# Scores of the last query tile made for both maps together, in two PSUM tiles

## The chip, the cores and the metric

The kernel runs on one core of a Trainium2 chip. The metric is the device time of one execution in microseconds (us), as the median of several runs. Five engines work side by side and wait for each other through semaphores: TensorE (PE in the profile; its weight loads are PEld), VectorE (DVE), ScalarE (ACT), GpSimd (POOL) and SyncE (SP), which issues most transfers.

## What is computed

Two transformer-like blocks over a sequence of 512 positions (528 with 16 meta tokens) of width 1024. The change is in the first block's differential attention: 8 heads, and in each head two softmax maps over the same values, with a key and a query of 64 channels for each map.

```python
def block(i):                       # i: a tile of 128 queries
    qb = lax.dynamic_slice_in_dim(qf, start, QB, axis=1)
    ...
    s = jnp.einsum('bqhmd,bkhmd->bhmqk', qb, kf)          # m: the map, d: 64 channels
    mask = cid[None, :] <= qc[:, None]
    p = jax.nn.softmax(jnp.where(mask, s, NEG_INF), axis=-1)
    a = p[:, :, 0] - lam * p[:, :, 1]
    return jnp.einsum('bhqk,bkhe->bqhe', a, vf)
```

Around it stand the projections that make queries, keys, values and gates, a causal convolution of 31 taps with a layer norm, output products, a feed-forward part, and then a second block of other mixers.

## The kernel before

All is held transposed: channels on partitions, positions along the free axis. The matrix products of the projections are the main stream of PE: units of 8 steps, and in a step 6 products (`step`, L560: three of the split weights by two column ranges of 256 to 264) accumulate into a tile `mm` of PSUM. There are two `mm` tiles. 56 such units make the first block's mixer, and the next weights are loaded and split into two parts (`wh` by ACT, `wl` by DVE) while a unit runs.

All else in the first mixer is side work. It is written as generators that run against a planner's clock (`self.pe`, and a lane each for DVE and ACT): after each step of the main stream `tick` resumes each generator whose time has come, and what it issues lands between two steps. The order is fixed when the program is built. A generator asks with `due` when its input will be ready by the plan and sleeps till then. A product in float32 is charged 4 columns in a cycle of 2.4 GHz by the plan (`mm`), whatever rows it uses. Operations of the convolution are taken from a list as DVE has room by the plan.

Side work has two PSUM tiles of 1024 columns, `at0` and `at1`. `at_get` hands out the one that is free by the plan, and `at_put` gives it back.

A head is two generators. `first` runs `softmax(i)` for the query tiles i = 0 to 3 (up to two ahead of use). `second` turns the values, and for each query tile combines the two maps (`weigh`), turns the result (`turn`, 128x128 blocks against `ident`) and multiplies with the values (`values`). Map 0 lies on partitions 0 to 63 of the queries and keys, map 1 on 64 to 127, so each score product uses 64 rows. For i = 0, 1 and 2 both maps fit into one tile: map m is written from column 512 m on, the product of map 0 and then that of map 1, and one memset and one reduction treat both. For i = 3 there are 528 key positions, which in two maps exceed one tile. There each map takes a tile by itself, with two products of 264 columns:

```python
for m in range(2):
    i_at, pt = yield from self.at_get()
    mm(pt[:, 248:512], q(m), k(m, 0, 264), True, True)
    mm(pt[:, 512:776], q(m), k(m, 264, 528), True, True)
    yield self.due(pt)
    V.memset(pt[0:64, 712:776], NEG)
    V.tensor_reduce(nb[:, m : m + 1], pt[:, 248:776], axis=AX.X, op=MAX, negate=True)
    yield self.due(nb)
    ex(m, pt[:, 248:776])
    self.at_put(i_at)
```

`ex` is the exponential on ACT with the row sum. In the profile the lines of DVE and ACT are all L158 (a helper), products are L314, and turns (products with `ident`) are L320; score products are `at<-act 64*128`, where 64 is the number of rows.

Of the kernel before, what the change touches and what calls it, by code (L numbers as in the profile page):

```python
# [52 lines left out]
def free(ap):  # L53
    n = 1
    for d in ap.shape[1:]:
        n *= d
    return n
# [105 lines left out]
class Build:  # L163
# [141 lines left out]
    def mm(self, out, lhsT, rhs, start=True, stop=True):  # L305
        n = free(rhs)
        if rhs.dtype == F32:
            c = max(0.213, n * 4 / 2400)
        elif rhs.dtype == F32R:
            c = max(0.107, n / 2400 + 0.003)  # L310
        else:
            c = max(0.03, n / 2400)
        self.pe_op(c, out, [lhsT, rhs])
        self.nc.tensor.matmul(out, lhsT, rhs, start=start, stop=stop)  # L314
# [448 lines left out]
    def attention(self, tp, h, qk, vs, ctx):  # L763


        V, S, mm, tr = self.V, self.S, self.mm, self.tr
# [3 lines left out]
        k = lambda m, a, b: kT[64 * m : 64 * m + 64, a:b]  # L770
        pair = lambda pt: pt.rearrange("p (a n) -> p a n", a=2)

        def softmax(i):
            L = 144 + 128 * i
            q = lambda m: qT[64 * m : 64 * m + 64, 2 + 128 * i : 130 + 128 * i]
            nb, l = self.sm(2, "nb"), self.sm(1, "ll")
            e = self.slot()

            def ex(m, sv):
                S.activation(e[:, m, :L], sv, AF.Exp, bias=nb[:, m : m + 1], accum_out=l if m else l0[:, i : i + 1])  # L780

            yield self.due(qT)
            if i < 3:
                i_at, pt = yield from self.at_get()
                for m in range(2):
                    mm(pt[:, 512 * m : 512 * m + L], q(m), k(m, 0, L))
                if i == 0:
                    for m in range(2):
                        mm(pt[0:2, 512 * m + 256 : 512 * m + 272], qT[64 * m : 64 * m + 64, 0:2], k(m, 0, 16))
                yield self.due(pt)  # L790
                V.memset(pair(pt)[0:64, :, L - 64 : L], NEG)
                if i == 0:
                    V.tensor_copy(sx[:, h, :, :], pair(pt)[0:2, :, 256:272])
                    if h == 7:
                        state["heads"] = True
                V.tensor_reduce(nb, pair(pt)[:, :, :L], axis=AX.X, op=MAX, negate=True)
                yield self.due(nb)
                for m in range(2):
                    ex(m, pt[:, 512 * m : 512 * m + L])
                self.at_put(i_at)  # L800
            else:
                for m in range(2):
                    i_at, pt = yield from self.at_get()
                    mm(pt[:, 248:512], q(m), k(m, 0, 264), True, True)
                    mm(pt[:, 512:776], q(m), k(m, 264, 528), True, True)
                    yield self.due(pt)
                    V.memset(pt[0:64, 712:776], NEG)
                    V.tensor_reduce(nb[:, m : m + 1], pt[:, 248:776], axis=AX.X, op=MAX, negate=True)
# [3 lines that stand above are left out]
            return e, l  # L812

        def first():
            for i in range(4):
                while i >= used[0] + 2:
                    yield 0.2
                made.append((yield from softmax(i)))
# [1384 lines left out]
```

## Time and profile before

| | |
|---|---|
| median of 3 runs | 1579.39 us (1579.03 to 1579.42) |
| the profiled execution | 1577.79 us |
| its span (first to last instruction) | 1576.0 us |
| granted TensorE clock, mean | 0.999 of full speed |
| PE busy | 1557.2 us, 99% |
| DVE busy | 1100.9 us, 70% |
| ACT busy | 680.3 us, 43% |
| 16 DMA engines, mean rate | 85 GB/s |

The busy time of PE is a union of instructions that overlap: one product is still draining when the next one starts. How long a product holds the engine is read from one start to the next, not from its own duration. The side work of the eight heads lies between 77 and 461 us of the span.

### The profile page before, as it was taken

To read this page: it belongs to the slowest core of one execution; us is meant where nothing else is said; L and a number is where in the kernel's file an instruction comes from. 1 tells how busy PE (TensorE), PEld (TensorE's weight loads), DVE (VectorE), ACT (ScalarE), POOL (GpSimd) and SP (SyncE) were. 2 spreads that over 40 slices of the span, in tenths; PEclk is the share of its full clock that TensorE was granted. 3 is DMA by queue.
4 is the path that set the end of the run, shared out by engine and by line. 5 is a ranking of instruction groups with operands and counts; after the bars stand their busy time and mean duration, and the time that the engine had idled before them with its cause. 6 is when DMAs were issued, how large, how long until landed. Compare 5 with 4: busy or idle time off the path is not lost.

```text
span 1576.0 us, 25330 instructions
## 1 busy us (share of the span) xinstructions
PE 1557.2 (99%) x10281; PEld 1392.9 (88%) x10281; DVE 1100.9 (70%) x2011; ACT 680.3 (43%) x1222; POOL 26.5 (2%) x89
## 2 busy tenths in 40 slices
PE   7999999999999999999999999999999999999998
PEld 6999999999999999999988877797799888888886
DVE  4989999897764667767643357899768877775224
ACT  5344444446843344444332222635566544444122
POOL 4000000000000000000000000000000000000000
PEclk9999999999999999999999999999999999999999
DMA  5322222222222333233333332231054133333221
GB/s 144 95 68 69 78 70 70 75 59 67 81 69 67 108 94 92 85 93 94 91 88 89 91 102 76 68 108 54 1 147 121 53 95 94 94 94 107 94 94 67
DMA packets 233005, 134.17 MB, mean 85 GB/s; under 512 B 6925, under 2 KB 228240, under 8 KB 232888
## 3 DMA queue, kind: packets, MB, share of 16 engines
q1 hardware_dynamic: 231448, 130.35, 28.5%
q8 instruction: 81, 1.33, 0.3%
q0 software_dynamic: 1136, 1.15, 0.3%
q10 hardware_dynamic: 304, 1.05, 0.2%
q14 instruction: 36, 0.29, 0.1%
HBM read 130.44 MB, written 2.10 MB: 84 GB/s over the span
## 4 chain that ended last, share of the span: by engine, by line
PE 97%; DVE 1%; ACT 1%; DMA 0%; issue 0%; DVEq 0%; ACTq 0%; POOLq 0%
PE mm L314 70%; PE at L314 25%; PE at L320 3%; ACT act L158 1%; DMA act<-in_x_dram 0%; DVE act L158 0%; DVE yy L158 0%; DVE yc L158 0%; ACT ys L158 0%; DVE wl L158 0%; DVE fx L158 0%; DVE res L158 0%; DVEq L2199 0%; ACT rsy L158 0%; DVE rsy L158 0%
## 5 line engine op out<-in xcount | busy, mean ns | idle before, releaser
L314 PE MATMUL mm<-act,wh 128*128 128x256 f32 (+3 forms) x4720 | 907.9, 306 | 1.3 <-ACT act L158 0.5
L314 PEld LDWEIGHTS mm<-act,wh 128*128 128x128 f32 (+1 forms) x4720 | 692.1, 189 | 50.5 <-issue 11.9
L314 PE MATMUL mm<-act,wl 128*128 128x256 f32 (+4 forms) x2360 | 562.6, 302 | 0.0
L158 DVE TENSOR_TENSOR wl<-raw,wh 128x1024 fp32r<-128x1024 f32 (+2 forms) x235 | 284.5, 1211 | 174.3 <-ACT wh L158 171.8
L158 ACT ACTIVATE wh<-raw 128x1024 fp32r<-128x1024 f32 (+2 forms) x235 | 245.7, 1047 | 371.4 <-PE mm L314 191.5
L314 PEld LDWEIGHTS mm<-act,wl 128*128 128x128 f32 (+1 forms) x2360 | 383.5, 189 | 18.0
L158 DVE SCALAR_TENSOR_TENSOR act<-u,par,act 128x514 f32<-128x514 f32 x232 | 161.2, 748 | 2.2 <-ACT act L158 2.2
L314 PE MATMUL at<-act,wh 128*128 128x512 f32 x416 | 129.6, 392 | 0.0
L314 PEld LDWEIGHTS at<-act,wh 128*128 128x128 f32 x416 | 78.0, 188 | 18.3
L314 PE MATMUL at<-wh,act 128*128 128x512 f32 x264 | 85.8, 394 | 0.0
L314 PE MATMUL mm<-wh,act 128*128 128x256 f32 (+1 forms) x344 | 84.6, 320 | 0.0
L314 PE MATMUL at<-act,act 128*128 128x256 f32 (+9 forms) x468 | 83.6, 329 | 0.7 <-ACT act L158 0.6
L314 PE MATMUL at<-act,wl 128*128 128x512 f32 x208 | 81.9, 394 | 0.0
L158 DVE TENSOR_TENSOR act<-act,act 128x514 f32<-128x514 f32 (+4 forms) x122 | 69.7, 590 | 9.0 <-ACT act L158 8.3
L314 PEld LDWEIGHTS at<-act,act 128*128 128x128 f32 (+1 forms) x468 | 60.3, 189 | 11.1 <-issue 5.0
L158 DVE SCALAR_TENSOR_TENSOR ft<-fx,par,ft 128x512 f32<-128x512 f32 x88 | 65.8, 749 | 1.5
L158 DVE TENSOR_TENSOR fx<-mm,rB 128x514 f32<-128x514 f32 x44 | 30.5, 694 | 51.3 <-PE mm L314 50.6
L158 ACT ACTIVATE act<-mm 128x528 f32<-128x528 f32 (+2 forms) x64 | 35.1, 548 | 71.7 <-PE mm L314 71.6
L314 PEld LDWEIGHTS mm<-wh,act 128*128 128x128 f32 x344 | 58.0, 189 | 7.2 <-issue 3.4
L158 DVE SCALAR_TENSOR_TENSOR gy<-gx,par,gy 128x512 f32<-128x512 f32 x84 | 62.6, 749 | 1.5
L158 ACT ACTIVATE act<-at 128x128 f32<-128x128 f32 (+6 forms) x88 | 34.3, 411 | 58.8 <-PE at L314 41.3
L314 PEld LDWEIGHTS at<-wh,act 128*128 128x128 f32 x264 | 49.6, 188 | 11.3
(286 smaller groups left out, 1450.7 us busy)
## 6 DMA issues: line engine op xcount, KB each, us to landing
raw<-in_w_in_dram SPq DMA_DIRECT2D x82, 512.0 KB, 3.8
raw<-in_w_up_dram SPq DMA_DIRECT2D x44, 512.0 KB, 3.8
raw<-in_ffn_up_dram SPq DMA_DIRECT2D x44, 512.0 KB, 3.8
raw<-in_ffn_down_dram SPq DMA_DIRECT2D x22, 512.0 KB, 3.3
raw<-in_w_out_dram SPq DMA_DIRECT2D x20, 512.0 KB, 4.5
raw<-in_w_down_dram SPq DMA_DIRECT2D x16, 512.0 KB, 3.8
raw<-in_w_conv_out_dram SPq DMA_DIRECT2D x8, 512.0 KB, 3.8
raw<-in_w_down_dram SPq DMA_DIRECT2D x8, 384.0 KB, 3.4
```

What stands on the lines that cost most here:

```text
L158: return f(*a, **k)
L314: self.nc.tensor.matmul(out, lhsT, rhs, start=start, stop=stop)
L320: self.nc.tensor.transpose(out, src, self.ident[p0 : p0 + k, p0 : p0 + k])
```

## The change

For i = 3 both `at` tiles are taken before the first product. Then the four products follow one another, the first 264 key positions of map 0, the same of map 1, the second 264 of map 0, of map 1. Mask, maximum and exponential are as before, for map 0 and then for map 1, and each tile is given back after its own exponential.

```diff
             else:
+                ats = []
                 for m in range(2):
-                    i_at, pt = yield from self.at_get()
-                    mm(pt[:, 248:512], q(m), k(m, 0, 264), True, True)
-                    mm(pt[:, 512:776], q(m), k(m, 264, 528), True, True)
+                    ats.append((yield from self.at_get()))
+                for c in range(2):
+                    for m in range(2):
+                        mm(ats[m][1][:, 248 + 264 * c : 512 + 264 * c], q(m), k(m, 264 * c, 264 * c + 264))
+                for m in range(2):
+                    i_at, pt = ats[m]
                     yield self.due(pt)
```

PE in head 0, around its last query tile, before (`at_1105` is map 0's tile, `at_1142` map 1's, `at_1121` the turn of query tile 2; a row of `wh` and one of `wl` are one step of six products):

```order
L314 MATMUL at_1105<-act_541 128x264 x2
L314 MATMUL mm_1062<-act_320,wh_876 128x264 x4
L314 MATMUL mm_1062<-act_320,wl_877 128x264 x2
L320 MATMUL at_1121<-ident,act_1028 128x128 x3
L320 MATMUL at_1121<-ident,act_1028 16x128
L314 MATMUL mm_1062<-act_335,wh_876 128x264 x4
L314 MATMUL mm_1062<-act_335,wl_877 128x264 x2
L314 MATMUL mm_1062<-act_356,wh_876 128x264 x4
L314 MATMUL mm_1062<-act_356,wl_877 128x264 x2
L314 MATMUL at_1142<-act_541 128x264 x2
L314 MATMUL at_1121<-vt_229,aT_233 128x128 x4
```

The same place after (`at_1106` is map 1's tile; the row that follows the last one here is the turn of query tile 2, into `at_1147`):

```order
L314 MATMUL at_1105<-act_541 128x264
L314 MATMUL at_1106<-act_541 128x264
L314 MATMUL at_1105<-act_541 128x264
L314 MATMUL at_1106<-act_541 128x264
L314 MATMUL mm_1062<-act_320,wh_876 128x264 x4
L314 MATMUL mm_1062<-act_320,wl_877 128x264 x2
L314 MATMUL mm_1062<-act_335,wh_876 128x264 x4
L314 MATMUL mm_1062<-act_335,wl_877 128x264 x2
L314 MATMUL mm_1062<-act_356,wh_876 128x264 x4
L314 MATMUL mm_1062<-act_356,wl_877 128x264 x2
L314 MATMUL mm_1062<-act_370,wh_876 128x264 x4
L314 MATMUL mm_1062<-act_370,wl_877 128x264 x2
```

Map 1's two products moved up to map 0's, and the turn of query tile 2 moved from 6 products behind map 0's scores to 24 products behind all four.

DVE and what it does to the scores in head 0, before (the rows of `u` are taps of the convolution):

```order
L158 SCALAR_TENSOR_TENSOR act_1028<-act_1028,kap_1109 128x400
L158 MEMSET at_1105 64x64
L158 TENSOR_REDUCE nb_1096<-at_1105 128x1
L158 SCALAR_TENSOR_TENSOR act_453<-u_801,par,act_453 128x514
L158 SCALAR_TENSOR_TENSOR act_738<-u_801,par,act_738 128x514
L158 SCALAR_TENSOR_TENSOR act_453<-u_801,par,act_453 128x514
L158 SCALAR_TENSOR_TENSOR act_738<-u_801,par,act_738 128x514
L158 SCALAR_TENSOR_TENSOR act_453<-u_801,par,act_453 128x514
L158 MEMSET at_1142 64x64
L158 TENSOR_REDUCE nb_1096<-at_1142 128x1
```

The same place of DVE after:

```order
L158 SCALAR_TENSOR_TENSOR act_1028<-act_1028,kap_1112 128x400
L158 SCALAR_TENSOR_TENSOR act_453<-u_801,par,act_453 128x514
L158 MEMSET at_1105 64x64
L158 TENSOR_REDUCE nb_1096<-at_1105 128x1
L158 SCALAR_TENSOR_TENSOR act_738<-u_801,par,act_738 128x514
L158 MEMSET at_1106 64x64
L158 TENSOR_REDUCE nb_1096<-at_1106 128x1
```

One tap moved ahead of map 0's mask and maximum, and map 1's follow map 0's after one tap instead of five.

ACT in head 0, after (before, three rows that read `at_1121` and three others stood between the two exponentials):

```order
L158 ACTIVATE act_916,ss_110_917<-act_916 128x128
L158 ACTIVATE act_1098,l_99_866<-at_1105,nb_1096 128x528
L158 ACTIVATE act_1154<-mm_1062 128x528
L158 ACTIVATE act_1098,ll_1097<-at_1106,nb_1096 128x528
L158 ACTIVATE aT_233<-at_1147 128x384
```

The emptying of `mm_1062` now stands between the two exponentials, and the copy of the turned tile behind both. In the eight heads the first turn after the four products stands 24, 30, 36, 36, 36, 30, 18 and 42 products of the main stream behind them. The places at which side work interrupts the main stream go from 107 to 105. Behind the last of attention's turns PE's order is the same in both.

## Rows read from the trace of the kernel before

**Rows 1.** The page: busy time by engine; share of the chain that ended last

```profile
PE 1557.2 (99%) x10281; PEld 1392.9 (88%) x10281; DVE 1100.9 (70%) x2011; ACT 680.3 (43%) x1222; POOL 26.5 (2%) x89
...
PE 97%; DVE 1%; ACT 1%; DMA 0%; issue 0%; DVEq 0%; ACTq 0%; POOLq 0%
```

**Rows 2.** Busy time in one stretch: start:end, then PE, PEld, DVE, ACT, POOL, clock

```profile
95.00:340.00 245.00, 245.00 (x1947) 230.68 (x1946) 224.12 (x439) 115.28 (x292) 0.62 (x5) 1.00 0.25 72
```

**Rows 3.** DVE's longest waits from 95 to 340: us, times, longest

```profile
DVE wl L158 <- ACT wh L158: 6.4, 8, 1.1
DVE at L158 <- PE at L314: 4.8, 8, 1.2
```

**Rows 4.** Score products by shape, whole span: count | busy us, mean ns

```profile
L314 PE MATMUL at<-act 64*128 64x264 f32 x64 | 18.5, 409 | 0.0
L314 PE MATMUL at<-act 64*128 64x400 f32 x32 | 7.5, 548 | 0.0
```

**Rows 5.** PE in order, tiles 1 and 2 of head 0: start, us, what

```profile
82.62 0.73 PE L314 MATMUL at<-act 64*128 64x272 f32 x4
83.28 0.76 PE L314 MATMUL mm<-act,wh 128*128 128x264 f32 x4
...
89.28 0.94 PE L314 MATMUL at<-act 64*128 64x400 f32 x4
90.15 0.55 PE L320 MATMUL at<-ident,act 128*128 128x128 f32 x3
```

**Rows 6.** PE, instructions running within 89.26 to 89.32, and within 94.94 to 95.00

```profile
89.28 0.61 PE L314 MATMUL at<-act 64*128 64x400 f32 x2
...
94.96 0.49 PE L314 MATMUL at<-act 64*128 64x264 f32 x1
```

**Rows 7.** PE in order, tile 3: the first and last of 16 groups

```profile
94.62 0.41 PE L314 MATMUL mm<-act,wl 128*128 128x264 f32 x2
94.96 1.15 PE L314 MATMUL at<-act 64*128 64x264 f32 x4
96.04 0.76 PE L314 MATMUL mm<-act,wh 128*128 128x264 f32 x4
...
446.01 1.16 PE L314 MATMUL at<-act 64*128 64x264 f32 x4
447.10 0.74 PE L314 MATMUL mm<-act,wh 128*128 128x256 f32 x4
```

**Rows 8.** PE in order, one undisturbed step of six products

```profile
102.17 0.41 PE L314 MATMUL mm<-act,wl 128*128 128x264 f32 x2
102.41 0.65 PE L314 MATMUL mm<-act,wh 128*128 128x264 f32 x4
102.90 0.40 PE L314 MATMUL mm<-act,wl 128*128 128x264 f32 x2
```

**Rows 9.** ACT and PE in order: head 0's and head 2's first group of tile 3

```profile
94.06 0.28 ACT L158 ACTIVATE act<-at 128x128 f32<-128x128 f32 x1
...
97.14 0.70 ACT L158 ACTIVATE act<-at,nb 128x528 f32<-128x528 f32 x1 [2.37 <-DVE nb L158]
...
187.84 1.15 PE L314 MATMUL at<-act 64*128 64x264 f32 x4
...
192.55 0.70 ACT L158 ACTIVATE act<-at,nb 128x528 f32<-128x528 f32 x1
```

**Rows 10.** DVE and PE in order, where attention and layer norm hand over

```profile
431.03 0.69 DVE L158 TENSOR_TENSOR act<-act,act 128x514 fp32r<-128x514 f32 x1 [0.98 <-ACT act L158]
...
458.45 0.69 DVE L158 SCALAR_TENSOR_TENSOR act<-act,mm 128x514 f32<-128x514 f32 x1
...
464.73 0.69 DVE L158 TENSOR_TENSOR act<-act,act 128x514 fp32r<-128x514 f32 x1
...
506.51 0.74 PE L314 MATMUL mm<-act,wh 128*128 128x256 f32 x4
```

## Prediction, before the changed kernel was run

> **What bounds the kernel now.** I read the page first: busy times and the chain that ended last. The reader is to see that PE is busy for 99% of the span and that 97% of the chain is PE [rows 1]. Then the stretch in which the changed scores lie: from 95 to 340 us PE is busy for all 245.00 us, DVE for 224.12, ACT for 115.28 [rows 2]. PE waits for nobody there, so whatever PE no longer has to do comes off the time, one for one, as long as nothing else becomes late. DVE is the runner-up, with 20.9 us idle; its longest waits are for a part of the weights that ACT makes and for scores from PE [rows 3]: at its idle places DVE is ahead.
>
> Then PE in order, for what a score product costs. The table by shape shows 64 instructions of 264 columns [rows 4] for 32 products (8 heads, 2 maps, 2 column ranges): a float32 product with 64 rows is two passes. Durations (409 ns) include draining, so I go from start to start.
>
> Query tiles 1 and 2 show two maps one after the other, four passes: 82.62 to 83.28 is 0.66 us for 272 columns, and 89.28 to 90.15 is 0.87 us for 400 [rows 5]. Tile 3 shows four passes too, but of one map: 94.96 to 96.04 is 1.08 us for 264 columns, and the last of the 16 such groups, 446.01 to 447.10, is 1.09 [rows 7]. So the narrower group takes longer. The two groups of rows 5 differ by 0.21 us for 128 columns, 1.64 ns a column, which leaves a fixed part of 0.66 - 272 x 0.00164 = 0.21 us. With that fixed part a pass of tile 3 is (1.08 - 0.21) / 4 = 0.2175 us, or 0.82 ns a column, half of 1.64. In the groups of two maps the four passes thus take the time of two: map 0 and map 1, on different halves of the rows, run at the same time. The cut of 60 ns says so directly: in it two instructions of tile 2 are running, but only one of tile 3 [rows 6].
>
> **The change part by part.** *The four products.* Before, a head has two groups, each 4 x 0.2175 + 0.21 = 1.08 us: 2.16. After, eight passes stand in one group, map by map in turn. If the maps overlap as in tiles 1 and 2, they make four layers: 4 x 0.2175 + 0.21 = 1.08. The same comes from stretching tile 2's group to the 528 columns a map has here: 0.87 + 128 x 0.00164 = 1.08. Saved: 1.08 us a head, 8.64 us in eight heads. No trace of before shows two products of each map in alternation at this width, so I bound it: with no overlap at all the group is 8 x 0.2175 + 0.21 = 1.95 and saves 0.21 a head, 1.7 us in all. I take the upper end, since the rows nearest to it (rows 5 and 6) overlap fully and differ only in that each map has one product.
>
> *Breaks in the main stream.* From the last `wl` pair to a score group it is 94.96 - 94.62 = 0.34 us, to the next step 102.41 - 102.17 = 0.24 [rows 7, 8], so going over to side work costs about 0.1, and I allow as much for the way back. By the order there are 105 such places instead of 107: 0.4 us saved, at most, since turns that shared a break with scores now make their own.
>
> *Both tiles held at once.* The scores hold both side tiles until the first exponential ends. Three things could now make PE wait. First, the second product needs the second tile, which ACT must have read. In head 0 that read, of a values product, ended at 94.06 + 0.28 = 94.34, and PE came to the scores at 94.96 [rows 7, 9]: 0.6 us to spare. Second, the turn that follows needs map 0's tile back. In head 0 map 0's exponential ended at 97.84, 2.88 us after the scores began [rows 7, 9]. The turn now stands 24 products behind them, and six products take 102.90 - 102.17 = 0.73 us [rows 8], so PE comes to it 1.08 + 24 x 0.122 + 0.1 = 4.1 us after they began: 1.2 to spare. In head 2 the exponential ended 193.25 - 187.84 = 5.41 us after [rows 9], against 1.08 + 36 x 0.122 + 0.1 = 5.6: 0.2 to spare, though there ACT worked on a turned tile before it which now comes after. The other six heads I did not list; with breaks of 18 to 42 products (3.4 to 6.3 us) I take them to lie between these two, 0.7 on average. Third, while PE waits everything behind it waits, the main stream included; while ACT's exponential of map 1 waits for DVE, the emptying of an `mm` tile can stand behind it, but PE has a second `mm` tile and 48 products (5.8 us) before it needs the first again. I cost all this at 0.4 us, which cancels the two breaks; bounds 0 and 2.5 us (every exponential 1 us later than before: 8 x 0.3).
>
> *Work that DVE and ACT do* is the same, instruction for instruction; only its place moves. The cover is DVE's idle time: heads 0 to 5 lie in the stretch of rows 2, so PE gets 6 x 1.08 = 6.5 us shorter there and DVE's 20.9 us of idle time become 14.4. DVE does not become the bound.
>
> *What comes next on PE.* The layer norm's last piece was written at 431.72; the first result that needs it was taken from PSUM from 458.45 on [rows 10]. By the order its products stand some 24 to 30 behind where they were (3.6 us) and PE is 8.6 us earlier: 12 of 26 us are used. Attention's last part was ready by 465.42, and the products that need it begin at 506.51 [rows 10]; its last turn moved back by 42 products, 5.1 us, out of 41. From there on the order is the same, and PE is the bound again. So the saving should reach the end.
>
> *Sum.* 1577.79 (profiled execution, span 1576.0 and 1.8 around it) - 8.6 - 0.4 + 0.4 = 1569.2. The runs' median lies 1.6 above the profiled execution, so the forecast for it is 1579.4 - 8.6 = 1570.8 us.
>
> **The rivals.** *A staircase.* Each product is two passes; if PE starts passes strictly in the order of the products, map 1's first pass can only run beside map 0's second. Eight passes then make five layers: 5 x 0.2175 + 0.21 = 1.30, saving 0.86 a head, 6.9 us: 1572.5. Against it: by the same rule tile 2's group would take three layers of 400 x 0.00082 = 0.328 and the fixed 0.21, 1.19 us, and it took 0.87 [rows 5]. The Trainium skill ("TensorE: Matmul & The Clock Gate", Part 3, The mechanism) says that products keep strict program order in start and end; with two passes to a product that is this staircase, and the trace speaks against it, unless the passes are interleaved before they reach the engine.
>
> *No overlap.* The change doesn't do what it says, for instance because the second product's own wait for its tile parts the maps. 1579.4 - 1.7 = 1577.7, within 0.2%. Against it is rows 6; for it, that no score product before had a wait in the middle of its group.
>
> *A wait for tiles takes the place.* PE runs through the scores sooner and comes to the turn before map 0's tile is free, in each head. With 0.7 us to spare on average, exponentials that end d us later cost 8 x (d - 0.7). At d = 1 that is 2.4 us: 1573.2. It eats the whole gain at d = 1.8, and from d = 2.2 on the kernel is over 0.2% slower; at d = 2.5 it is 14.4 - 8.6 = 5.8 us slower, 1585.2. What speaks for it is DVE at 91% [rows 2], with a tap now ahead of map 0's mask in head 0, and that the planner still charges the four products as if they ran one by one, so PE comes sooner than planned. Against it: one tap is 0.6 to 0.7 us, and map 0's second product is done as long after the group's start as before. The Trainium skill ("TensorEngine Tiling (Array Packing)", PSUM Bottleneck) warns of just this, that packing speeds up the products but not the emptying of PSUM. Nothing in the trace shows it here so far, as PE waits for nobody.
>
> **How the numbers follow.** Forecast, full overlap with at most 1 us of waits: 76%, 1570.8. Some of it given back by waits (1572 to 1576): 9%. Staircase, 1572.5: 6%. No overlap, 1577.7: 5%. Tiles, slower: 4%. The low end is the forecast with no wait at all and 1 us for the spread of runs and profile: 1570.8 - 0.4 - 1.0 = 1569.4; I put it at 1569.2. The high end takes in the staircase and waits up to 3.5 us: 1574.3. A measurement can tell about 0.2% (3.2 us) from no change, so faster means under 1576.2: 0.90; same 0.06; slower 0.04.
>
> **What would show it.** In the profile after, one group of eight passes of 264 columns in each head, 1.08 us from its start to the next start (1.30 for the staircase, 1.95 without overlap); two instructions running in its first 60 ns; PE's busy time about 8 us less, DVE's and ACT's the same; no new wait of PE before products or turns of `at` tiles. I am wrong if groups are short but the span is not, which would put the loss into waits of PE behind them, or if the groups themselves stay long.

## The result and the profile after

The changed kernel takes 1568.26 us (median of 4 runs, 1567.50 to 1568.26), against 1579.24 us of the kernel before beside it (4 runs, 1579.03 to 1579.42). The ratio is 0.9932, with a 95% interval of 0.992 to 0.9944: 10.98 us, or 0.7%, faster. The forecast was 1570.8 with a range from 1569.2 to 1574.3. The direction and the mechanism of the main term were right, but the time is 2.5 us below the forecast and 0.9 us below the range: two small terms and the place of tiles in SBUF had been left out or mis-sized.

The profiled execution took 1567.50 us, with a span of 1565.7 (before: 1577.79 and 1576.0). Its page answers to [rows 1]:

```profile
PE 1546.3 (99%) x10279; PEld 1386.4 (89%) x10281; DVE 1101.5 (70%) x2011; ACT 680.5 (43%) x1222; POOL 25.9 (2%) x89
...
PE 97%; DVE 1%; ACT 1%; DMA 0%; issue 0%; DVEq 0%; ACTq 0%; POOLq 0%
```

PE's busy time fell by 10.9 us, those of DVE and ACT stayed within 0.6 us, and PE still holds 97% of the chain that ended last. The stretch of the scores answers to [rows 2] (start:end, length, then PE, PEld, DVE, ACT, POOL, clock):

```profile
95.00:340.00 245.00, 244.92 (x2001) 233.26 (x2000) 228.34 (x449) 118.34 (x298) 0.62 (x5) 1.00 0.25 72
```

In the same 245 us PE starts 54 more products (2001 for 1947), and DVE does 4.2 us more; its idle time falls from 20.9 to 16.7 us. Its waits there, of which the two for scores answer to the eight in [rows 3] (us in all, times, longest):

```profile
DVE act L158 <- ACT act L158: 4.0, 6, 1.4
DVE wl L158 <- ACT wh L158: 3.3, 6, 1.2
DVE at L158 <- PE at L314: 1.2, 2, 0.9
```

From 80 to 465 us, the whole of the side work, the list of waits has no row of PE. That list shows no idle time below 0.15 us, and there is one such wait: in head 5 PE comes to the turn behind the scores before ACT's exponential has left map 0's tile (PE, then ACT):

```profile
333.43 0.40 PE L314 MATMUL mm<-act,wl 128*128 128x264 f32 x2
333.91 0.66 PE L320 MATMUL at<-ident,act 128*128 128x128 f32 x4
...
333.06 0.70 ACT L158 ACTIVATE act<-at,nb 128x528 f32<-128x528 f32 x1 [3.65 <-DVE nb L158]
```

From the pair of `wl` to the turn it is 0.48 us there, and 0.24 in the heads without a wait, so this one costs 0.24 us. It is also in the second trace of the same kernel.

The score products by shape answer to the first line of [rows 4]. Their number and mean are the same (64, 408 ns for 409). Their busy time, in which overlapping products count once, halved from 18.5 to 9.3 us:

```profile
L314 PE MATMUL at<-act 64*128 64x264 f32 x64 | 9.3, 408 | 0.0
```

PE in order, head 0, around the group that was made of the two (start, us, what), and what runs in the first 60 ns of that group. These answer to [rows 6, 7]:

```profile
95.21 0.41 PE L314 MATMUL mm<-act,wl 128*128 128x264 f32 x2
95.55 1.16 PE L314 MATMUL at<-act 64*128 64x264 f32 x8
96.64 0.76 PE L314 MATMUL mm<-act,wh 128*128 128x264 f32 x4
97.25 0.40 PE L314 MATMUL mm<-act,wl 128*128 128x264 f32 x2
97.48 0.65 PE L314 MATMUL mm<-act,wh 128*128 128x264 f32 x4
97.97 0.41 PE L314 MATMUL mm<-act,wl 128*128 128x264 f32 x2
...
99.42 0.41 PE L314 MATMUL mm<-act,wl 128*128 128x264 f32 x2
99.66 0.60 PE L320 MATMUL at<-ident,act 128*128 128x128 f32 x4
100.02 0.74 PE L314 MATMUL mm<-act,wh 128*128 128x264 f32 x4
100.59 0.41 PE L314 MATMUL mm<-act,wl 128*128 128x264 f32 x2
...
95.55 0.49 PE L314 MATMUL at<-act 64*128 64x264 f32 x2
```

Eight passes take 96.64 - 95.55 = 1.09 us, as long as four took in [rows 7], and two are running at once from the start.

**Where the 10.3 us of the span went.** I cut both traces at fixed products of the main stream, which has 7080 of them in the same order, and took the times from start to start:

| stretch of the main stream | before, us | after, us | difference |
|---|---|---|---|
| start to its 400th product (loading) | 78.67 | 79.28 | +0.6 |
| 400th to 2900th (first mixer, with all changed scores) | 395.13 | 384.91 | -10.2 |
| 2900th to 5500th (after the mixer, mostly feed-forward) | 317.27 | 316.27 | -1.0 |
| 5500th to the last | 651.99 | 652.08 | +0.1 |
| behind the last | 132.96 | 133.16 | +0.2 |

The first line is loading, which varied between 78.67 and 80.05 us over the executions profiled here. The second and third lines are what has to be explained: 8.6 us were forecast for the second, none for the third.

The 10.2 us, from the starts of single products: 16 groups of 1.085 us became 8 of 1.091, which is 8.63 us. Before a score product of any tile that follows a main product there is a gap from start to start of 213 ns on average, instead of 121 between two main products. There were 39 such places and there are 31: 8 x 92 ns = 0.74 us. The first main product behind a break holds PE for 205 ns (behind turns and values) to 226 ns (behind scores), also instead of 121. Such long products went from 108 to 104; one of those gone had no side work ahead of it, but stood 0.35 us in the kernel before, at 458.85. Together 0.5 us. Against these stands the wait in head 5, 0.24 us. About 0.6 us is left, in small differences of turns and steps whose cause is not traced.

### The profile page after: what moved, and what is told of

Its sections match the earlier page's. It is cut to its first block, busy times and chain, and to the rows that moved or that the text cites. A ratio compares the mean times of both kernels' runs of the same rounds, so it can differ in the third digit from the quotient of the medians.

```text
span 1565.7 us, 25299 instructions
## 1 busy us (share of the span) xinstructions
PE 1546.3 (99%) x10279; PEld 1386.4 (89%) x10281; DVE 1101.5 (70%) x2011; ACT 680.5 (43%) x1222; POOL 25.9 (2%) x89
## 3 DMA queue, kind: packets, MB, share of 16 engines
q0 software_dynamic: 1136, 1.15, 0.3%
## 4 chain that ended last, share of the span: by engine, by line
PE 97%; DVE 1%; ACT 1%; DMA 0%; issue 0%; DVEq 0%; ACTq 0%; POOLq 0%
PE mm L314 70%; PE at L314 24%; PE at L320 3%; ACT act L158 1%; DVE act L158 0%; DMA act<-in_x_dram 0%; DVE yy L158 0%; DVE wl L158 0%; ACT ys L158 0%; DVE yc L158 0%; ACT wh L158 0%; DVE nb L158 0%; DVE fx L158 0%; DVE res L158 0%; ACT e L158 0%
## 5 line engine op out<-in xcount | busy, mean ns | idle before, releaser
L314 PEld LDWEIGHTS mm<-act,wh 128*128 128x128 f32 (+1 forms) x4720 | 692.0, 189 | 49.5 <-issue 10.9
```

## The experiments

Times of these runs are medians beside runs of the kernel before on the same chip. The stage lengths are those of the table's second and third lines, and the "pace" is the length of 2000 products, from the 3500th to the 5500th. In all kernels ten small products and one short wait stand between them, the same 1.8 us together in each, and no other side work.

**The same kernel again.** Is the 1.0 us behind the mixer a spread between executions?

> The changed kernel once more, beside the kernel before on the same chip. Of the 11.0 us by which the medians differ, the traces place 10.2 us in the first mixer (8.6 us of overlapping passes, 0.7 us of going over to score groups, the rest shorter breaks); the other 0.8 us lie behind it, where both kernels do the same. Theory: those 0.8 us are spread from one execution to the next, so the difference here may be anything from 10 to 11 us, and the time of a main-stream product behind the mixer (120.5 ns before, 120.0 after) will differ between profiles of the same kernel. Rival: something the change does to the weights' loads makes the rest faster, then the 0.8 us and the 120.0 ns come again.

1568.43 us (5 runs; the kernel before 1578.94 in 12), ratio 0.9932 (0.9919 to 0.9944). The mixer took 384.97 us and the pace was 242.38, as in the first trace of this kernel, to 0.01 us, against 243.42 in the kernel before. So it is no spread between executions, and that explanation of mine fell.

**Both maps' products on the same rows.** Map 0's queries and keys are used for both maps, so map 1's scores of the last query tile are left out; everything else stands where it stands in the changed kernel.

```diff
-  mm(ats[m][1][:, 248 + 264 * c : 512 + 264 * c], q(m), k(m, 264 * c, 264 * c + 264))
+  mm(ats[m][1][:, 248 + 264 * c : 512 + 264 * c], q(0), k(0, 264 * c, 264 * c + 264))
```

> The changed kernel with both maps' last-tile scores computed from map 0's queries and keys (this leaves map 1's scores of that tile out). Order, tiles, waits and sizes are those of the changed kernel; only the rows of the array are the same for all four products. Theory (the gain is the overlap of two maps on different rows): the eight passes come one after another, the group is 8 x 0.2175 + 0.21 = 1.95 us instead of 1.09, and the kernel is 8 x 0.86 = 6.9 us slower than the changed one: about 1575.2, still 4 us faster than before. Rival (the gain is the new order of the side work): same time as the changed kernel, 1568.3.

1575.03 us (8 runs), ratio 0.9974 (0.9964 to 0.9985): 6.6 us above the changed kernel, from a forecast of 6.9. PE in order, the same place, and the products by shape:

```profile
95.18 0.41 PE L314 MATMUL mm<-act,wl 128*128 128x264 f32 x2
95.52 2.04 PE L314 MATMUL at<-act 64*128 64x264 f32 x8
97.49 0.75 PE L314 MATMUL mm<-act,wh 128*128 128x264 f32 x4
...
L314 PE MATMUL at<-act 64*128 64x264 f32 x64 | 16.4, 395 | 0.0
```

As many products in the same order, and the group takes 1.97 us instead of 1.09. It is the two halves of the rows that let the maps overlap. Eight groups times 0.88 us is 7.1; the mixer grew by 6.8 us, since the longer groups leave the exponentials more time and the wait of head 5 (0.24 us) is gone. Without overlap the kernel is still 3.9 us faster than the kernel before. In its trace, whose span is 2.8 us shorter, the mixer gives 3.4 us (395.13 to 391.70), from eight fixed parts and eight breaks fewer, and the stage behind it 1.0; loading took 0.6 us longer there and the rest of the program 1.1.

**Map by map.** All of map 0's products, then all of map 1's, in one group.

```diff
-                for c in range(2):
-                    for m in range(2):
+                for m in range(2):
+                    for c in range(2):
                         mm(ats[m][1][:, 248 + 264 * c : 512 + 264 * c], q(m), k(m, 264 * c, 264 * c + 264))
```

> The changed kernel with the four products in the order map 0, map 0, map 1, map 1. Theory A (the engine starts a pass as soon as its rows are free, and can pass over products that wait for other rows): full overlap, group 1.09 us, 1568.3. Theory B (products start in program order, and overlap only with the neighbour): map 0's last pass beside map 1's first, seven layers, 7 x 0.2175 + 0.21 = 1.73 us, 8 x 0.64 = 5.1 us slower than the changed kernel: 1573.4. No overlap at all would give 1.95 us and 1575.2.

1568.27 us (5 runs), ratio 0.993 (0.9918 to 0.9943), the same as the changed kernel. PE in order, and what runs in the first 60 ns of the group:

```profile
95.14 0.41 PE L314 MATMUL mm<-act,wl 128*128 128x264 f32 x2
95.48 1.17 PE L314 MATMUL at<-act 64*128 64x264 f32 x8
96.58 0.64 PE L314 MATMUL mm<-act,wh 128*128 128x264 f32 x3
...
95.48 0.50 PE L314 MATMUL at<-act 64*128 64x264 f32 x2
```

The group takes 1.10 us and two passes run from its start, the second one 13 ns behind the first (7 ns in the changed kernel). On the same rows a second pass starts 327 ns behind the first, so this one is map 1's, although four passes of map 0 stand ahead of the first of map 1 in the program. So the alternation, which the change's name speaks of, is not what gives the time: that both maps stand in one group does. The staircase of my first rival, which is what a strict order of starts would give, is refuted from this side as well. The Trainium skill ("TensorE: Matmul & The Clock Gate", Part 3, The mechanism) has products start and end in strict program order; for float32 products of two passes on two halves of the rows, this trace doesn't agree.

**Two groups of two products.** A step of the main stream between the first and the second pair.

```diff
                     for m in range(2):
                         mm(ats[m][1][:, 248 + 264 * c : 512 + 264 * c], q(m), k(m, 264 * c, 264 * c + 264))
+                    if c == 0:
+                        yield 0.05
```

> The changed kernel with one step of the main stream between the first pair of products and the second. Theory (a group of scores has a fixed part of 0.21 us, and going over to it costs 0.09 us more and the first main product behind it 0.10 more, because the array goes from 128 rows to 64 and back): each head has two groups of 2 x 0.2175 + 0.21 = 0.645 us, 0.2 us more in sum, and 0.19 us for the second entry and exit: 8 x 0.39 = 3.2 us slower than the changed kernel, 1571.4. Rival (breaks of the main stream are free, as my forecast nearly had it): 8 x 0.2 = 1.6 us, 1569.9, or nothing at all.

1568.74 us (5 runs), ratio 0.9935 (0.9922 to 0.9949). I missed by 2.7 us. PE in order:

```profile
94.90 0.41 PE L314 MATMUL mm<-act,wl 128*128 128x264 f32 x2
95.24 0.72 PE L314 MATMUL at<-act 64*128 64x264 f32 x4
95.89 0.76 PE L314 MATMUL mm<-act,wh 128*128 128x264 f32 x4
96.48 0.41 PE L314 MATMUL mm<-act,wl 128*128 128x264 f32 x2
96.82 0.72 PE L314 MATMUL at<-act 64*128 64x264 f32 x4
97.47 0.64 PE L314 MATMUL mm<-act,wh 128*128 128x264 f32 x3
```

Two groups of 0.65 us instead of one of 1.09: 0.21 us more, the fixed part of a group. Going over (0.34 us from the pair of `wl` to the scores, instead of 0.24) and coming back add the rest. The mixer grew by 388.16 - 384.91 = 3.2 us, or 0.41 for each of 8 further groups, which is what was forecast for it. (PE's wait in head 5 is not in this kernel either, so the groups by themselves cost a little more.) But the stage behind the mixer, which this edit doesn't touch, became 1.8 us shorter (314.44 for 316.27), and most of the loss was gone. The price of a further score group is shown; that a total can hide it is shown as well.

**What sets the pace behind the mixer.** The programs of before and after have the same order there, and it takes 243.42, 242.38 and, with two groups, 240.72 us. In the built programs, the tiles that move through PE there come out of a pool of 30 slots, and land in other slots when side work takes and returns them in another order. From before to after, three quarters of the 2000 products read their moving tile from another slot, while the weights lie where they lay. A slot is 2 x 528 x 4 = 4224 bytes, an odd multiple of 128. Four kernels move them without touching the order. Each pad is one line (this one is 128 bytes on each partition, [P, 64] is 256):

```diff
+        pool("pad", 1).tile([P, 32], F32, name="pad")
         self.act = pool("act", 30)
```

and, to move the weights along with them:

```diff
+        pool("pad", 1).tile([P, 32], F32, name="pad")
         self.wp = pool("wp", 3)
```

The kernel before again, without a pad, and with 128 bytes ahead of the pool of moving tiles:

> The kernel before once more, with a profile of its own. In the profiles so far the 2000 products of the main stream from number 3500 to 5500 (first feed-forward, the same work and order in every kernel) took 243.4 us in the kernel before, 242.4 in the changed one, in its repetition and in the two variants that place their tiles alike, and 240.7 in the variant with two groups. If that goes with the built kernel, 243.4 comes again here; if it is spread between executions, another value comes.

> The kernel before with 128 unused bytes for each partition ahead of its pool of working tiles, so that all these tiles lie 128 bytes higher in SBUF beside the weights, whose place stays. Order, waits and sizes are unchanged. Theory (the pace of the main stream depends on where its moving tiles lie): products 3500 to 5500 take another time than 243.4 us, by half a us or more, and the kernel's time moves with it. Rival (the pace comes from something else, such as the timing of the other engines' work): 243.4 us and the time of the kernel before.

Without a pad 1578.81 us, ratio 1.0002 (0.9993 to 1.0011), pace 243.39: it goes with the build. With it 1576.61 us, ratio 0.9988 (0.9979 to 0.9997), pace 240.71, the one of the two groups. The changed kernel with 128 and with 256 bytes:

> The same 128 bytes in the changed kernel. Theory: products 3500 to 5500 take another time than 242.4 us, the groups of scores in the first mixer stay at 1.09 us and the stretch of the mixer about 10.2 us shorter than in the kernel before with the same bytes. Rival: 242.4 us and 1568.3 again.

> The changed kernel with 256 unused bytes instead of 128. Theory: a third pace of the main stream. Rival: 242.4 us and 1568.3 again.

With 128 bytes it takes 1566.02 us (1565.95 to 1567.09, 5 runs), ratio 0.9922 (0.991 to 0.9935), the fastest kernel of this study; its pace is 241.78. With 256 bytes it takes 1567.8, ratio 0.9933 (0.992 to 0.9945), and the pace is 242.38, just that without a pad. I had expected a third pace there; that it comes back after 256 bytes was a miss that told something. And the kernel before with the weights moved along:

> The kernel before with the 128 unused bytes ahead of the weights' pool instead of behind it: weights and working tiles both lie 128 bytes higher, their distance is that of the kernel before. With only the working tiles moved, products 3500 to 5500 took 240.7 us instead of 243.4. Theory A (the pace hangs on where moving tiles and weights lie relative to each other): 243.4 us again and the time of the kernel before, 1578.7. Theory B (it hangs on the working tiles' own addresses, or theirs relative to something that did not move): 240.7 us and 1576.6.

1578.93 us (11 runs), ratio 1.0001 (0.9992 to 1.001), pace 243.42, as without a pad. So it is neither the address of the moving tiles by itself nor the pad: it is where they lie against the weights. That 256 bytes bring the pace back was tried on the changed kernel only, and moving both on the kernel before only. The feed-forward part by its 44 emptyings on DVE (duration in ns, first and last start in us), of before, before with 128 bytes, before with both moved, after, after with 128 bytes, after with 256 bytes, and two groups:

```profile
L158 DVE TENSOR_TENSOR fx<-mm,rB x44: 686/694/695, 554.8 to 799.5; 128x514 f32<-128x514 f32 x44
...
L158 DVE TENSOR_TENSOR fx<-mm,rB x44: 687/694/695, 555.5 to 797.3; 128x514 f32<-128x514 f32 x44
...
L158 DVE TENSOR_TENSOR fx<-mm,rB x44: 686/694/695, 555.5 to 800.1; 128x514 f32<-128x514 f32 x44
...
L158 DVE TENSOR_TENSOR fx<-mm,rB x44: 684/694/695, 545.3 to 788.8; 128x514 f32<-128x514 f32 x44
...
L158 DVE TENSOR_TENSOR fx<-mm,rB x44: 687/694/697, 545.0 to 787.9; 128x514 f32<-128x514 f32 x44
...
L158 DVE TENSOR_TENSOR fx<-mm,rB x44: 685/694/695, 545.8 to 789.3; 128x514 f32<-128x514 f32 x44
...
L158 DVE TENSOR_TENSOR fx<-mm,rB x44: 685/693/695, 548.0 to 789.9; 128x514 f32<-128x514 f32 x44
```

Last minus first: 244.7, 241.8, 244.6, 243.5, 242.9, 243.5 and 241.9 us, and each emptying lasts 693 to 694 ns in the median throughout, so that it is PE whose pace differs. Apart from the two stops named above, a step of six products takes 708 to 751 ns, in a pattern that comes again to 1 ns, step by step, in two traces of one build, and is another one in another build; in the two builds with the pace 240.7 no step is above 725. Why a step is longer at one relative place than at another, the trace doesn't say. That stays open.

The pads also give the change's own worth apart from this: with 128 bytes in both, the mixer goes from 394.73 to 384.55, 10.2 us, as without pads, and the stage behind it from 314.83 to 315.52, 0.7 us the other way.

**The same idea elsewhere.** In the second block's sparse attention two heads lie on the two halves of the rows as well. On top of 128 bytes of pad, two heads now take both tiles, make their scores together and then go on as two generators.

```diff
-                i, pt = yield from self.at_get()
-                o = pt[:, :L]
-                mm(o, B["aq"][hp][r64, t * P : t * P + P], B["ak"][hp][r64, :L], True, t == 0)
+                ats = []
+                for m in range(2):
+                    ats.append((yield from self.at_get()))
+                for m in range(2):
+                    r64 = slice(64 * m, 64 * m + 64)
+                    mm(ats[m][1][:, :L], B["aq"][hp][r64, t * P : t * P + P], B["ak"][hp][r64, :L], True, t == 0)
...
+                self.start(sparse(t, 2 * hp + 1, *ats[1]))
+                yield from sparse(t, 2 * hp, *ats[0])
+                yield from wait(f"sp{4 * t + 2 * hp + 1}")
```

> The changed kernel with the 128 bytes ahead of its working tiles, and the same idea in the second block's sparse attention: two heads that lie on different halves of the rows make their scores together in two tiles, then their masks, instead of each head by itself (16 products of 128 to 512 columns in 8 pairs). Theory (what counts is that two maps on different rows follow one another): at 0.82 ns a column and pass, 2 passes, the 8 products that are now covered hold PE for 2 x 2 x 0.00082 x (128 + 256 + 384 + 512) = 4.2 us, of which the trace shows the two pairs of 128 columns partly covered already (0.2 to 0.4 us less), and each pair goes over to 64 rows once less (0.1 us each): about 4 to 5 us less than the 1566.0 us of the kernel with the bytes alone, 1561 to 1562. Rival (in the second block the pairs wait for each other's masks or tiles): gain under 2 us, 1564 or more.

1575.74 us (11 runs), ratio 0.9979 (0.997 to 0.9988): 9.7 us slower than the padded kernel without it, which ran on another chip (9.5 if each is taken against the kernel before beside it). The time that the theory forecast was missed, and the rival had no price for a loss. But the overlap itself came: from start to start the 32 passes of these scores hold PE for 6.0 us instead of 11.2; 4 to 5 us less were forecast. Mixer and feed-forward are as in the padded kernel (384.54 and 315.52 us); the loss lies in 50 us of the second block. First the padded kernel, then this one, from 1100 to 1150 us, and this one in smaller cuts (columns as in [rows 2]):

```profile
1100.00:1150.00 50.00, 48.51 (x350) 40.71 (x351) 33.54 (x86) 26.80 (x58) 0.21 (x2) 1.00 0.14 38
...
1100.00:1150.00 50.00, 39.22 (x264) 33.74 (x264) 27.27 (x76) 21.38 (x49) 0.21 (x2) 0.84 0.08 22
...
1128.00:1136.00 8.00, 1.65 (x12) 1.17 (x10) 6.05 (x23) 4.34 (x6) 0.00 (x0) 0.88 0.00 0
1136.00:1144.00 8.00, 4.08 (x16) 3.30 (x16) 6.70 (x10) 1.55 (x3) 0.00 (x0) 0.50 0.31 86
1144.00:1150.00 6.00, 5.66 (x25) 5.07 (x25) 0.75 (x1) 0.51 (x1) 0.00 (x0) 0.50 0.21 62
1150.00:1160.00 10.00, 9.51 (x75) 9.31 (x75) 4.26 (x5) 6.43 (x12) 0.00 (x0) 0.95 0.34 98
```

PE's waits in those 50 us, and PE in order at the longest:

```profile
PE at L321 <- DVE act L158: 7.6, 2, 6.4
PE mm L315 <- DVE act L158: 2.9, 2, 2.7
...
1128.52 0.60 PE L321 MATMUL at<-ident,act 128*128 128x128 f32 x4
1135.47 0.69 PE L321 MATMUL at<-ident,act 128*128 128x128 f32 x2 [6.35 <-DVE act L158]
```

A turn stands in PE's queue 6.4 us ahead of what DVE makes for it, and products of the main stream stand behind it. What DVE works on meanwhile isn't a mask or an emptying of these scores. It is the normalization of another mixer, a chain of small operations, each on the result of the one before. Here are its start and its end in this kernel, and then its start in the padded one, where it stands 12.7 us earlier:

```profile
1130.58 0.25 DVE L158 RECIPROCAL rd<-den 128x16 f32<-128x16 f32 x1
1133.79 0.17 DVE L158 TENSOR_TENSOR rd<-rd,rsy 128x16 f32<-128x16 f32 x1
...
1117.89 0.25 DVE L158 RECIPROCAL rd<-den 128x16 f32<-128x16 f32 x1
```

While PE waits, the granted clock falls to 0.50, the lower of its two levels (1.2 GHz), and it stays there from 1136 to 1150, so that the work right after the wait runs at half speed. The edit also changed how many heads run at once (a generator waits for both of its heads), and with it the order of the side work; which part of it made that chain late, this run doesn't tell. What it shows is that overlapping products can come true and the program still lose, when the edit that brings them together moves other side work to where PE has to wait for it.

## Why the prediction came out as it did

**What bounds the kernel: right.** Busy PE time that was taken away came off one for one. PE's busy time fell by 10.9 us and the span by 10.3.

**The four products: right.** 1.08 us was forecast for the joined group and 1.091 measured; 8.64 us in all, and 8.63 measured. The price without overlap (1.95) was measured too: 1.97. The way to it, from tiles 1 and 2 of the same head [rows 5] and the cut of 60 ns [rows 6], carried.

**Breaks in the main stream: failed, by its count.** The step took each place at which side work interrupts the main stream as equal, some 0.1 us in and 0.1 out, and found 105 instead of 107 of them: 0.4 us at most. In the trace after, the price hangs on what PE goes over to. From the pair of `wl` to scores it is 95.55 - 95.21 = 0.34 us, and the step behind them takes 97.25 - 96.64 = 0.61 us to its own `wl` pair instead of 0.49 (97.97 - 97.48). From `wl` to a turn it is 99.66 - 99.42 = 0.24, as to any main product, and the step behind it takes 0.57. So the way in costs something where PE goes from products of 128 rows to products of 64 (and as much at three places in the mixer where turns or products of 2 or 16 rows follow), and the count that matters is that of score groups behind a main product: 8 fewer, not 2 fewer. That gave 0.74 us on the way in and, with one stall that went, 0.5 us on the way back. The two groups say the same from the other side, with 0.41 us for each further group (0.21 of it inside). The rows I read [rows 7, 8] held the 0.1 us; a third row, of the way into a turn, would have told that it isn't a price of breaks in general.

**Both tiles held at once: the wait was real, its place and size were not those forecast.** 0.4 us of waits was put in, and with it the saving at the breaks was cancelled. Measured is one wait of 0.24 us. The narrow place was to be head 2, with 0.2 us forecast between the end of map 0's exponential and the turn. ACT and PE in order there, after:

```profile
186.65 1.16 PE L314 MATMUL at<-act 64*128 64x264 f32 x8
...
190.23 0.70 ACT L158 ACTIVATE act<-at,nb 128x528 f32<-128x528 f32 x1
...
192.24 0.60 PE L320 MATMUL at<-ident,act 128*128 128x128 f32 x4
```

The exponential ends 4.3 us after the scores began, not 5.4 as before [rows 9], since the work on a turned tile that stood ahead of it now comes after; 1.3 us are to spare. The prediction named this effect and didn't put it into the number. The wait came in head 5, one of the six heads that the prediction did not list. There the exponential ended 4.92 us after the scores began, instead of 3.86 before, and the turn, 30 products behind the scores, was due at 4.8; in head 1 there were 0.2 us to spare. Over the eight heads the exponential ends 3.0 to 4.9 us after the group's start. (The plan charges a float32 product four cycles of 2.4 GHz a column, not four columns a cycle as the description of the kernel has it: 1.76 us for the four products that PE does in 1.09, so PE does come sooner than planned.) In the sum both steps stood against each other at zero, and measured they are -1.6 us together: -0.74 and -0.5 at the breaks, +0.24 for the wait, and the -0.6 in small differences.

**"From there on the order is the same ... so the saving should reach the end": the conclusion held, the premise failed.** Nothing was given back. But the same order took 1.0 us less in the stage behind the mixer. The reading that is left is that the tiles that move through PE lie elsewhere against the weights: the built programs show that they do, and the pads show that this alone moves the stage by as much. No row of before could have given the size. That an edit of side work changes which slot later tiles get could have been seen from the program, and would have asked for a range wider by a microsecond or two: builds with the same order differ by up to 2.8 us in this stage (314.44 to 317.27).

**The sum.** Profiled: 1569.2 forecast, 1567.5 measured. The difference of -1.7 is -1.6 (breaks and waits), -1.0 (placement), and +0.9 that lies in loading and at the end. For the median I took 1.6 us between profile and median, from three runs; it was 0.8 here, which is the rest of the 2.5.

**The rivals.** The staircase fell by the group's length and by the kernel in which map 0 goes first. No overlap fell by the group's length; the kernel on the same rows shows what it would have given, 1575.0 (forecast for that rival: 1577.7, without what the breaks give). Waits that take the place came in the first mixer in one head, by just the mechanism of the third rival, and cost 0.24 us. Longer ones came where the idea was tried again, in the second block, but by another mechanism: PE stood in a queue ahead of another mixer's normalization on DVE, not of a tile of the scores. The Trainium skill ("TensorEngine Tiling (Array Packing)", PSUM Bottleneck) warns that packing speeds up products and not what empties them. In the first mixer the trace shows little of this, with PE at 244.92 of 245 us and the wait of 0.24 us for an exponential that reads the scores out of their tile; in the second block the longest wait, 6.4 us, is not for an emptying of the scores.

## What to carry to other kernels

Where two products use different halves of the rows, put them into one group on PE, in whatever order, and leave no other work between them. Here each separate group of 64-row products cost 0.41 us beside its passes, about as much as the overlap of one pair of products of 264 columns saves (2 x 0.2175 us). Before you do it, look which waits end next in that stage, and after it check that the edit has not moved other side work to where PE waits for it. A list of waits can leave out short ones: go through the gaps from start to start as well. And compare two builds stage by stage, between fixed products, before you believe a difference of a few microseconds in the total: other slots for the same tiles alone moved a stage here by up to 1%.

## What the runs showed of the hardware that I had not expected

**The pace of the main stream depends on where its operands lie against each other.** 2000 products in the same order took 240.7 to 243.4 us, to 0.03 us the same in each trace of a build. A shift of the moving tiles by 128 bytes changed it (243.42 to 240.71, 242.38 to 241.78), a shift by 256 bytes (changed kernel) didn't, and a shift of tiles and weights together by 128 (kernel before) didn't. The cause inside the chip is not shown.

**Passes on one half of the rows don't wait for those on the other half that stand ahead of them in the program.** With all of map 0 first, map 1 began 13 ns behind it, and the group took 1.10 us for 1.09.

**Going over from 128-row products to 64-row products costs 0.1 us (213 ns from start to start for 121), and to turns of 128 rows next to nothing (125 ns on average).** The first 128-row product behind scores holds PE for 226 ns, behind turns and values for 205, and otherwise for 121.
